# Weight sums of the Strassen pairs: additions alone, and two of the four made by DMA in the feed-forward

## The chip, the cores and the metric

One core of one Trainium2 chip. The metric is the device time of one execution in microseconds, the median of three. Matrix work runs on TensorE (PE), elementwise work on VectorE (DVE) and ScalarE (ACT); GpSimd (POOL) and SyncE (SP) mostly issue DMAs. All data is float32.

## The reference

One layer of a hybrid encoder over a prompt of 512 rows and 8 sample streams of 16 rows (T = 640 rows together, 1024 columns): three gated branches are merged, and a SwiGLU feed-forward of width 2816 follows. The part that matters here:

```python
z = x @ w_in                                  # among its columns: the gates of the branches
g = jax.nn.sigmoid(gates + b_gate)
x = layer_norm(ALPHA * x + merged @ w_out, ln1_g, ln1_b)
ffn = (jax.nn.silu(x @ w_ffn_gate) * (x @ w_ffn_up)) @ w_ffn_down
x = layer_norm(ALPHA * x + ffn, ln2_g, ln2_b)
```

## The kernel before, in words

Activations lie transposed in SBUF, 128 features by rows, split for precision into a high part `xh` (fp32r) and a low part `xl`. A weight block is split the same way just before use: ACT copies the high part, DVE subtracts it from the block to get the low part. Each product is then three matmuls: high by high, high by low, low by high.

**The work as a list of steps.** The program is one list `steps`, written out in a fixed order. A step has a weight part, its matmuls (`mm`), an evacuation, and work to be done ahead of it (`before`). The order of the code sets the order on each engine: for step i the high part of step i + 2 is copied, `before` runs, the matmuls run, and between them come the evacuation of step i - 1 and the low split of step i + 2. Weight loads of 1 MB (`Load`) go out on the SP queue into two buffers `wr`. The next load is issued when the low split of the last step that reads the old buffer is in the program, and it waits on the chip for that split.

**Strassen pairs.** Two column blocks of a weight matrix (256 columns, one load) make a `Pair`. Its 1024 by 256 block is cut in four quarters 11, 12, 21, 22 (128 partitions by 512 elements each) and the activations in four as well. Seven products m1, m6, m2, m7, m5, m4, m3 of 12 matmuls each (128x320) take the place of eight. They need four sums of weight quarters, t1 to t4, each 128x512, and four sums of activations, s1 to s4. DVE forms the weight sums of a pair while the pair before it is multiplied: t3 and t2 (`sums_1`) ahead of step 2, t1 and t4 (`sums_2`) ahead of step 3 (one step later in the first pair of a run of pairs). The products gather in PSUM: m6 and m7 share a bank, and m6's value is read by DVE between the two (`after`).

Eight pairs make gates of the branches (`gate_pairs`), and twenty make the feed-forward: for each two blocks a "gate" pair (`through`, Silu on ACT) and an "up" pair (`times`, a multiplication on DVE). `seven` writes the seven steps of a pair, `pair_steps` a run of pairs. Below, the twenty are counted from 0. Temporary tiles come from 53 slots of 128x640 in a first-in, first-out list (`get`, `free`).

`Engine` only counts assumed times, for the order of side work; in the feed-forward pairs there is none. L66 is the line that records every operation of PE, ACT and DVE, so instructions are told by their tiles: `wr` the load's buffer, `wh` and `wl` the split blocks (two buffers in turn, each with both parts), `pu` PSUM, `s` any slot.

Of the kernel before, what the change touches and what calls it, by code (L numbers as in the profile page):

```python
# [11 lines left out]
OP = mybir.AluOpType  # L12
# [133 lines left out]
def trunk(ctx, tc, x_prompt, x_sample, mem_t, rows_a, rows_b, hist_b, cache_k, cache_v, ln_in_g, ln_in_b, w_in,  # L146
# [69 lines left out]
    class Load:  # L216
        def __init__(self, shape, ap, users):
            self.shape, self.ap, self.left, self.tile = shape, ap, users, None
            loads.append(self)
# [1168 lines left out]
    def sums_stream(in_place=None, given=None):  # L1388

        quarters.clear()  # L1390
        for n, (t0, k0) in QUARTERS.items():
            quarters[n] = tuple([x[:, k0 + k, t0:t0 + HT] for k in range(half)] for x in (xh, xl))
        a = {}

        def whole(n, i):
            t0, k0 = QUARTERS[n]
            if given is not None:
                a[n, i] = given.pop((t0 // HT, (k0 + i) // 2))
                return
            a[n, i] = get([128, 2, HT])  # L1400
            V.tensor_tensor(a[n, i], *(f32(x[:, k0 + i:k0 + i + 2, t0:t0 + HT]) for x in (xh, xl)), op=OP.add)

        def mix(out, p, q, i, op=OP.subtract):
            V.tensor_tensor(a[out, i], a[p, i], a[q, i], op=op)

        def part(n, q, keep=False):

            at = [], []
            for i in blocks:
                hi, lo = get([128, 2, HT], F32R), get([128, 2, HT], F32R)  # L1410
                split(hi, lo, a[q, i])
                if not keep:
                    free(a.pop((q, i)))
                sums.extend((hi, lo))
                for to, y in zip(at, (hi, lo)):
                    to.extend(y[:, k] for k in range(2))
                yield "v"
            quarters[n] = at
            made.add(n)

        blocks = range(0, half, 2)
        for i in blocks:
            whole("22", i)
            whole("21", i)
            yield "v"
            mix("22", "21", "22", i, OP.add)
            whole("11", i)
            yield "v"
            mix("21", "11", "21", i)
            mix("11", "22", "11", i)  # L1430
            yield "v"
        yield from part("s2", "11", True)
        if in_place is None:
            yield from part("s1", "22")
        yield from part("s3", "21")
        for i in blocks:
            whole("12", i)
            yield "v"
            mix("12", "12", "11", i)
            free(a.pop(("11", i)))  # L1440
            yield "v"
        yield from part("s4", "12")
        if in_place is not None:
            while not in_place():
                yield None
            for i in blocks:
                split(*(y[:, i:i + 2, HT:] for y in (xh, xl)), a["22", i])
                free(a.pop(("22", i)))
                yield 1
            quarters["s1"] = quarters.pop("21")  # L1450
            made.add("s1")
# [14 lines left out]
    class Pair:  # L1466


        def __init__(self, ld):
            self.ld, self.t = ld, {}  # L1470

        def block(self, n):
            if n[0] == "t":
# [1 line left out]
            i, j = int(n[0]) - 1, int(n[1]) - 1  # L1475
            return self.ld.tile[:, j, half * i:half * (i + 1)]

        def add(self, n, p, q, op):
            self.t[n] = get([128, half, 128])
            V.tensor_tensor(self.t[n], self.block(p), self.block(q), op=op)  # L1480

        def sums_1(self):
            self.add("t3", "22", "12", OP.subtract)
            self.add("t2", "t3", "11", OP.add)

        def sums_2(self):
            self.add("t1", "12", "11", OP.subtract)
            self.add("t4", "t2", "21", OP.subtract)

        def drop(self, n):  # L1490
            if n in self.t:
# [4 lines left out]
                ("m3", "z", False, "s4", "22"))  # L1496
    parity = [0]

    def seven(pair, put, following, first=False):

        acc, tmp, late = {}, {}, []

        def fourth(p):
            put(0, 1, p, tmp["b"][:, 0], OP.subtract)

        def fifth(p):
            put(1, 1, p, tmp["b"][:, 0], OP.add)
            if first:
                V.tensor_tensor(tmp["a"][:, 1], tmp["a"][:, 1], p, op=OP.add)

        def after(n, p):
            if n == "m1":
                tmp["a"], tmp["b"] = get([128, 2, HT]), get([128, 2, HT])
                copy(tmp["a"][:, 0], p)
            elif n == "m6":
                V.tensor_tensor(tmp["a"][:, 1], tmp["a"][:, 0], p, op=OP.add)
            elif n == "m2":
                put(0, 0, p, None, None)
            elif n == "m7":
                V.tensor_tensor(tmp["b"][:, 0], tmp["a"][:, 0], p, op=OP.add)  # L1520
                for f in late:
                    f()
            elif n in ("m4", "m5"):
                f = lambda: (fourth if n == "m4" else fifth)(p)
                if first:
                    late.append(f)
                else:
                    f()
            else:
                free(tmp["b"])  # L1530
                put(1, 0, p, tmp["a"][:, 1], OP.add)
                free(tmp["a"])

        products = PRODUCTS
        if first:

            products = [PRODUCTS[i] for i in (0, 5, 2, 1, 4, 3)] + [("m3", "x", True, "s4", "22")]
        for i, (n, u, opens, xn, wn) in enumerate(products):
            def mm(w, u=u, opens=opens, xn=xn):
                if opens:  # L1540
                    acc[u] = pu(1)[0][:, :HT]
                p = acc[u]
                hi, lo = w
                xhi, xlo = quarters[xn]
                for k in range(half):
                    P.matmul(p, hi[:, k], xhi[k], start=opens and k == 0, stop=False, skip_group_check=not opens)
                    P.matmul(p, hi[:, k], xlo[k], start=False, stop=False, skip_group_check=not opens)
                yield
                for k in range(half):
                    P.matmul(p, lo[:, k], xhi[k], start=False, stop=k == half - 1, skip_group_check=not opens)  # L1550
                yield

            before = None
            if first:
                wanted = "s1" if i == 1 else xn if xn[0] == "s" else None
                ahead = following and {3: following.sums_1, 4: following.sums_2}.get(i)
                before = lambda wanted=wanted, ahead=ahead: (wanted and sums_for(wanted), ahead and ahead())
            elif following and not first and i == 2:
                before = following.sums_1
            elif following and not first and i == 3:  # L1560
                before = following.sums_2
            Step(pair.ld, (lambda r, wn=wn: pair.block(wn)), [128, half, 128], mm,
                 (lambda n=n, u=u: after(n, acc[u])), before=before, half=parity[0] % 2,
                 after=lambda wn=wn: pair.drop(wn))
            parity[0] += 1

    def pair_steps(pairs, start=True):

        early = steps[-2]
        ahead = early.before  # L1570
        early.before = lambda: (ahead and ahead(), pairs[0][0].sums_1(), pairs[0][0].sums_2())
        for i, (pair, put) in enumerate(pairs):
            seven(pair, put, pairs[i + 1][0] if i + 1 < len(pairs) else None, start and i == 0)

    def w_load(w, col, users):
        return Load([128, 2, KD, 128], lambda: blocks_of(w[col // 256], 2), users)
# [1 line left out]
    def through(function, to, ready=None, **how):  # L1578

        def put(j, c, p, x, op):  # L1580
            row = to(j)
            h = c2(row)[:, c]
            if x is not None:
                V.tensor_tensor(h, x, p, op=op)
            A.activation(h, p if x is None else h, function, **{n: f(j) for n, f in how.items()})
            if ready and j != c:
                ready(j, row)
        return put
# [256 lines left out]
    def times(m2):  # L1845

        def put(j, c, p, x, op):
            h = c2(hT[m2 + j])[:, c]
            y = p
            if x is not None:  # L1850
                y = get([128, HT])
                V.tensor_tensor(y, x, p, op=op)
            V.tensor_tensor(h, h, y, op=OP.mult)
            if x is not None:
                free(y)
        return put

    pairs = []
    for m2 in range(2, KF, 2):
        pairs.append((Pair(w_load(w_ffn_gate, m2 * 128, 7)),  # L1860
                      through(AF.Silu, lambda i, m2=m2: slot_of(hT, m2 + i))))
        pairs.append((Pair(w_load(w_ffn_up, m2 * 128, 7)), times(m2)))
    pair_steps(pairs)
    for k in range(2):
        assert steps[-5 + k].before is None
# [279 lines left out]
```

## Time and profile before

| | before |
|---|---|
| median of 3 runs | 1041.67 us (1041.48 to 1042.96) |
| profiled execution | 1041.37 us, span 1039.6 us |
| granted TensorE clock | 0.997 |
| POOL's share of the span | 10% |
| moved by DMA | 142.00 MB, 137 GB/s mean |
| feed-forward pairs | about 628 to 884 us of the span |

Times in the trace are microseconds from the span's start. A row of the order of time reads: start, duration, engine, line, operation, out<-in, shapes, count, and in brackets the idle time before it with what ended it. Matmuls are pipelined, so each shows a longer duration than the distance to the next. A row of DMA issues reads: queue, count, KB, and the us from issue to landing.

### The profile page before, as it was taken

What the parts mean: (1) busy time and instruction counts of PE and PEld (TensorE: products, weight loads), DVE (VectorE), ACT (ScalarE), POOL (GpSimd) and SP (SyncE); (2) the same over time, 40 slices, a digit from 0 to 9 for tenths busy, and PEclk for the clock granted to TensorE, in tenths of its full rate; (3) what the DMA queues carried; (4) which work ended last, traced back from release to release, by engine and by line L of the source; (5) the groups of instructions that cost most, each with busy time, mean ns of one, the idle gap of its engine ahead of it and who ended that gap; (6) DMA issues with size and microseconds to landing.
All of it is one profiled execution on the core that took longest, in us unless ns stands there. A gap on an engine that the chain in (4) does not pass through costs nothing.

```text
span 1039.6 us, 16847 instructions
## 1 busy us (share of the span) xinstructions
PE 1028.0 (99%) x6641; PEld 978.2 (94%) x6641; DVE 819.2 (79%) x1452; ACT 517.2 (50%) x938; POOL 99.9 (10%) x176
## 2 busy tenths in 40 slices
PE   9999999999999999999999999999999999999997
PEld 6999999999999999999998899999999999888886
DVE  5769899899953969898785579888888887576875
ACT  5723564356579686755322455444444334344350
POOL 1000403110100010101021210000000001000111
PEclk9999999999999999999999999999999999999998
DMA  9722215641240154844566222222222223833581
GB/s 350 256 89 82 79 61 174 220 162 62 92 169 24 42 183 157 203 107 151 186 241 218 102 102 81 82 82 81 81 85 95 101 87 115 310 122 122 183 283 41
DMA packets 34590, 142.00 MB, mean 137 GB/s; under 512 B 4656, under 2 KB 5488, under 8 KB 24656
## 3 DMA queue, kind: packets, MB, share of 16 engines
q1 hardware_dynamic: 23472, 104.84, 28.8%
q0 software_dynamic: 11040, 36.10, 10.6%
q8 instruction: 52, 0.85, 0.3%
q14 instruction: 26, 0.21, 0.1%
HBM read 120.55 MB, written 20.36 MB: 136 GB/s over the span
## 4 chain that ended last, share of the span: by engine, by line
PE 94%; DVE 3%; ACT 1%; issue 1%; DMA 1%; DVEq 0%; POOL 0%; POOLq 0%; SPq 0%
PE pu L66 83%; PE pv L66 11%; DVE s L66 2%; ACT s L66 1%; DMA wr<-in_w_in 1%; DVE wl L66 1%; DVE wh L66 0%; DVE xres L66 0%; ACT wh L66 0%; ACT L66 0%; DVEq L2141 0%; ACT xh L66 0%; ACT wl L66 0%; DVE st L66 0%; ACT hout L66 0%
## 5 line engine op out<-in xcount | busy, mean ns | idle before, releaser
L66 ACT ACTIVATE wh<-wr 128x1024 fp32r<-128x1024 f32 (+1 forms) x147 | 130.1, 888 | 200.0 <-PE pu L66 100.8
L66 PE MATMUL pu<-xh,wh 128*128 128x320 f32 x976 | 228.9, 310 | 0.5 <-ACT xh L66 0.5
L66 PE MATMUL pu<-xh,wl 128*128 128x320 f32 x976 | 227.7, 309 | 0.1
L66 PE MATMUL pu<-s,wh 128*128 128x320 f32 x1136 | 196.4, 309 | 1.1 <-ACT s L66 1.0
L66 PE MATMUL pu<-xl,wh 128*128 128x320 f32 x792 | 193.7, 309 | 0.0
L66 DVE TENSOR_TENSOR s<-s,s 128x640 f32<-128x640 f32 (+5 forms) x206 | 144.2, 721 | 46.8 <-ACT s L66 44.3
L66 PEld LDWEIGHTS pu<-s,wh 128*128 128x128 f32 x1136 | 174.0, 188 | 1.8 <-ACT s L66 1.3
L66 PEld LDWEIGHTS pu<-xh,wh 128*128 128x128 f32 x976 | 164.9, 188 | 2.4 <-issue 1.0
L66 PEld LDWEIGHTS pu<-xh,wl 128*128 128x128 f32 x976 | 165.4, 188 | 0.4 <-DVE wl L66 0.4
L66 PE MATMUL pu<-s,wl 128*128 128x320 f32 x880 | 158.6, 309 | 1.1 <-DVE s L66 1.1
L66 DVE TENSOR_TENSOR wl<-wr,wh 128x1024 fp32r<-128x1024 f32 (+1 forms) x105 | 119.2, 1138 | 48.3 <-ACT wh L66 48.3
L66 PEld LDWEIGHTS pu<-s,wl 128*128 128x128 f32 x880 | 136.3, 188 | 1.8 <-issue 1.1
L66 PEld LDWEIGHTS pu<-xl,wh 128*128 128x128 f32 x792 | 136.4, 188 | 0.0
L66 DVE TENSOR_TENSOR s<-s,pu 128x320 f32<-128x320 f32 x192 | 91.1, 485 | 51.1 <-PE pu L66 47.7
L66 ACT ACTIVATE s<-s 128x640 fp32r<-128x640 f32 (+4 forms) x148 | 89.3, 627 | 79.1 <-DVE s L66 77.5
L66 DVE SCALAR_TENSOR_TENSOR s<-s,pb,s 128x511 f32<-128x511 f32 (+14 forms) x240 | 111.9, 533 | 5.8 <-ACT s L66 5.8
L66 PE MATMUL pu<-wh,s 128*128 128x512 f32 x364 | 106.7, 382 | 0.0
L66 PEld LDWEIGHTS pu<-wh,s 128*128 128x128 f32 x364 | 67.0, 188 | 13.3 <-issue 0.5
L66 ACT ACTIVATE s<-pu 128x320 f32<-128x320 f32 (+2 forms) x110 | 44.3, 437 | 64.0 <-PE pu L66 63.4
L66 PE MATMUL pu<-s,s 128*128 128x512 f32 (+1 forms) x236 | 61.8, 413 | 0.0
L66 PE MATMUL pu<-wl,s 128*128 128x512 f32 x182 | 57.1, 381 | 0.0
L66 PEld LDWEIGHTS pu<-s,s 128*128 128x128 f32 x236 | 43.1, 190 | 14.0 <-issue 7.0
(127 smaller groups left out, 1203.3 us busy)
## 6 DMA issues: line engine op xcount, KB each, us to landing
wr<-in_w_in SPq DMA_DIRECT2D x26, 1024.0 KB, 4.9
wr<-in_w_ffn_down SPq DMA_DIRECT2D x19, 1024.0 KB, 4.8
wr<-in_w_ffn_gate SPq DMA_DIRECT2D x11, 1024.0 KB, 4.8
wr<-in_w_ffn_up SPq DMA_DIRECT2D x11, 1024.0 KB, 4.7
m<-s POOLq DMA_DIRECT2D x16, 320.0 KB, 4.9
s<-in_cache_k POOLq DMA_DIRECT2D x16, 256.0 KB, 5.3
s<-in_cache_v POOLq DMA_DIRECT2D x16, 256.0 KB, 5.0
wr<-in_proj_a SPq DMA_DIRECT2D x4, 1024.0 KB, 5.5
```

Source lines behind the costliest of these rows:

```text
L66: return f(*a, **k)
```

## The change

The sums are written so that all four weight sums are additions (t3 = 22 + 12, t2 = t3 + 11, t1 = 12 + 11, t4 = t2 + 21). For that some signs change sides: in the activation sums and in the evacuations, where the PSUM operand now comes first.

In the feed-forward, for every pair but the first, t3 and t1 are no longer formed by DVE. `fetch` loads quarters 22 and 11 once more from memory into the slots of t3 and t1 (SP queue, 256 KB each). `gather` then adds quarter 12 to each by an accumulating DMA (POOL queue, 256 KB each). `sums_1` and `sums_2` skip what is there, so t2 = t3 + 11 and t4 = t2 + 21 stay on DVE at their places. `fetch` of pair i + 2 stands ahead of step 5 of pair i, `gather` ahead of its step 6; those of pair 1 stand three and two steps ahead of pair 0.

```diff
     class Pair:
...
-        def add(self, n, p, q, op):
+        def add(self, n, p, q):
+            if n in self.t:
+                return
             self.t[n] = get([128, half, 128])
-            V.tensor_tensor(self.t[n], self.block(p), self.block(q), op=op)
+            V.tensor_tensor(self.t[n], self.block(p), self.block(q), op=OP.add)
+
+        def in_memory(self, n):
+            i, j = int(n[0]) - 1, int(n[1]) - 1
+            return self.ld.ap()[:, j, half * i:half * (i + 1)]
+
+        def fetch(self):
+            for n, q in (("t3", "22"), ("t1", "11")):
+                self.t[n] = get([128, half, 128])
+                S.dma_start(self.t[n], self.in_memory(q))
+
+        def gather(self):
+            for n in ("t3", "t1"):
+                G.dma_start(self.t[n], self.in_memory("12"), accum_op=OP.add)
 
         def sums_1(self):
-            self.add("t3", "22", "12", OP.subtract)
-            self.add("t2", "t3", "11", OP.add)
+            self.add("t3", "22", "12")
+            self.add("t2", "t3", "11")
 
         def sums_2(self):
-            self.add("t1", "12", "11", OP.subtract)
-            self.add("t4", "t2", "21", OP.subtract)
+            self.add("t1", "12", "11")
+            self.add("t4", "t2", "21")
...
-    def seven(pair, put, following, first=False):
+    def seven(pair, put, following, first=False, second=None):
...
         def fourth(p):
-            put(0, 1, p, tmp["b"][:, 0], OP.subtract)
+            put(0, 1, p, tmp["b"][:, 0], OP.add)
...
+            wanted = (("s1" if i == 1 else xn if xn[0] == "s" else None) if first else None)
+            ahead = []
+            if following:
+                ahead += {2 + first: [following.sums_1], 3 + first: [following.sums_2]}.get(i, [])
+            if second:
+                ahead += {5: [second.fetch], 6: [second.gather]}.get(i, [])
             before = None
...
+            if wanted or ahead:
+                before = lambda wanted=wanted, ahead=ahead: (wanted and sums_for(wanted), [f() for f in ahead])
...
+        pairs += [(None, None)] * 2
+        pre = pairs[1][0].summed
+        earlier(3, *([pairs[1][0].fetch] if pre else []))
+        earlier(2, pairs[0][0].sums_1, pairs[0][0].sums_2, *([pairs[1][0].gather] if pre else []))
...
-                V.tensor_tensor(h, x, p, op=op)
+                V.tensor_tensor(h, p, x, op=op)
...
-        pairs.append((Pair(w_load(w_ffn_gate, m2 * 128, 7)),
+        pairs.append((Pair(w_load(w_ffn_gate, m2 * 128, 7), True),
...
-        pairs.append((Pair(w_load(w_ffn_up, m2 * 128, 7)), times(m2)))
+        pairs.append((Pair(w_load(w_ffn_up, m2 * 128, 7), True), times(m2)))
```

On DVE, in pair 5, from the sums for pair 6 to the low split of m3. Before (the numbers behind `s` are the slot and a running count; in brackets the engines and DMA queues, HW for SP and SW for POOL, that the instruction waits for):

```order
L66 TENSOR_TENSOR s27_513_7763<-wr_7682 128x512 [waits DMAHW2_49]
L66 TENSOR_TENSOR s48_514_7765<-s27_513_7763,wr_7682 128x512 [waits DVE_49]
L66 TENSOR_TENSOR s7_511_7753<-s7_511_7753,pu_7744 128x320 [waits PE_49,Activation_49]
L66 TENSOR_TENSOR wl_7761<-s5_507_7650,wl_7761 128x512 [waits Activation_49]
L66 TENSOR_TENSOR s4_515_7783<-wr_7682 128x512
L66 TENSOR_TENSOR s47_516_7785<-s48_514_7765,wr_7682 128x512 [waits DVE_49]
L66 TENSOR_TENSOR s24_509_7662<-s24_509_7662,pu_7726 128x320 [waits PE_49]
L66 TENSOR_TENSOR wh_7781<-s6_508_7652,wh_7781 128x512 [waits Activation_49]
L66 TENSOR_TENSOR s51_512_7754<-s7_511_7753,pu_7744 128x320 [waits PE_49]
L66 TENSOR_TENSOR wl_7801<-wr_7547,wl_7801 128x512 [waits Activation_49]
```

and now:

```order
L66 TENSOR_TENSOR s47_515_7779<-s48_510_7700,wr_7692 128x512 [waits DMAHW4_49,DMASW3_49]
L66 TENSOR_TENSOR s51_513_7769<-s51_513_7769,pu_7760 128x320 [waits PE_49,Activation_49]
L66 TENSOR_TENSOR wl_7777<-s13_501_7565,wl_7777 128x512 [waits DMASW2_49,Activation_49]
L66 TENSOR_TENSOR s44_516_7797<-s47_515_7779,wr_7692 128x512 [waits DVE_49]
L66 TENSOR_TENSOR s24_509_7672<-s24_509_7672,pu_7742 128x320 [waits PE_49]
L66 TENSOR_TENSOR wh_7795<-s38_508_7662,wh_7795 128x512 [waits Activation_49]
L66 TENSOR_TENSOR s36_514_7770<-s51_513_7769,pu_7760 128x320 [waits PE_49]
L66 TENSOR_TENSOR wl_7813<-wr_7555,wl_7813 128x512 [waits Activation_49]
```

The first rows of t3 and t1 (`s27` and `s4` from `wr` alone) are gone. t2 (`s48` before, `s47` now) waits for the accumulating DMA besides its weight load. It still stands ahead of the read of m6 (`s7` before, `s51` now, from `pu`). The read of m7 and, last, m3's low split from `wr` keep their places.

On the SP queue, from the load of pair 4 on, before:

```order
L255 DMA wr_7415<-in_w_ffn_gate 128x2048 [waits DMAHW6_49,DVE_49]
L255 DMA wr_7547<-in_w_ffn_up 128x2048 [waits DMAHW7_49,DVE_49]
L255 DMA wr_7682<-in_w_ffn_gate 128x2048 [waits DMAHW0_49,DVE_49]
L255 DMA wr_7814<-in_w_ffn_up 128x2048 [waits DMAHW1_49,DVE_49]
L255 DMA wr_7949<-in_w_ffn_gate 128x2048 [waits DMAHW2_49,DVE_49]
```

and now, from the load of pair 4 to that of pair 7:

```order
L255 DMA wr_7421<-in_w_ffn_gate 128x2048 [waits DMAHW6_49,DMAHW0_49,DVE_49]
L1491 DMA s1_493_7429<-in_w_ffn_gate 128x512 [waits DMASW3_49,DMASW2_49]
L1491 DMA s31_494_7431<-in_w_ffn_gate 128x512
L255 DMA wr_7555<-in_w_ffn_up 128x2048 [waits DMAHW3_49,DMAHW1_49,DVE_49]
L1491 DMA s41_500_7563<-in_w_ffn_up 128x512 [waits DMAHW2_49]
L1491 DMA s13_501_7565<-in_w_ffn_up 128x512
L255 DMA wr_7692<-in_w_ffn_gate 128x2048 [waits DMAHW6_49,DMAHW4_49,DVE_49]
L1491 DMA s48_510_7700<-in_w_ffn_gate 128x512 [waits DMAHW5_49]
L1491 DMA s0_511_7702<-in_w_ffn_gate 128x512 [waits Pool_49]
L255 DMA wr_7826<-in_w_ffn_up 128x2048 [waits DMAHW7_49,DMAHW1_49,DVE_49]
```

Each pair's two fetches stand directly behind its own weight load. On POOL, where nothing stood between the last store of x1 and the load of the residual, there are now 38 accumulations:

```order
L1495 DMA s1_493_7429<-in_w_ffn_gate 128x512 [waits DMAHW7_49,DMASW7_49,DVE_49]
L1495 DMA s31_494_7431<-in_w_ffn_gate 128x512 [waits DMAHW0_49,DMASW0_49,DVE_49]
L1495 DMA s41_500_7563<-in_w_ffn_up 128x512 [waits DMAHW2_49,DMASW1_49,DVE_49]
L1495 DMA s13_501_7565<-in_w_ffn_up 128x512 [waits DMAHW3_49,DMASW2_49,DVE_49]
L1495 DMA s48_510_7700<-in_w_ffn_gate 128x512 [waits DMAHW5_49,DMASW3_49,DVE_49]
L1495 DMA s0_511_7702<-in_w_ffn_gate 128x512 [waits DMAHW6_49,DMASW4_49,DVE_49]
```

Each waits for its fetch (DMAHW). The order on PE and the number of instructions on ACT stay as they were.

More of the change, by code (lines that the diff above doesn't have):

```diff
@@ L1425, in sums_stream @@
             yield "v"
-            mix("22", "21", "22", i, OP.add)
+            mix("22", "21", "22", i)
             whole("11", i)
@@ L1438, in sums_stream @@
             yield "v"
-            mix("12", "12", "11", i)
+            mix("12", "12", "11", i, OP.add)
             free(a.pop(("11", i)))
@@ L1466, in trunk, with __init__ @@
     class Pair:
-        def __init__(self, ld):
-            self.ld, self.t = ld, {}
+        def __init__(self, ld, summed=False):
+            self.ld, self.t, self.summed = ld, {}, summed
         def block(self, n):
@@ L1497, in trunk @@
     parity = [0]
-    def seven(pair, put, following, first=False):
+    def seven(pair, put, following, first=False, second=None):
         acc, tmp, late = {}, {}, []
         def fourth(p):
-            put(0, 1, p, tmp["b"][:, 0], OP.subtract)
+            put(0, 1, p, tmp["b"][:, 0], OP.add)
         def fifth(p):
-            put(1, 1, p, tmp["b"][:, 0], OP.add)
+            put(1, 1, p, tmp["b"][:, 0], OP.subtract)
             if first:
-                V.tensor_tensor(tmp["a"][:, 1], tmp["a"][:, 1], p, op=OP.add)
+                V.tensor_tensor(tmp["a"][:, 1], tmp["a"][:, 1], p, op=OP.subtract)
         def after(n, p):
@@ L1530, in after @@
                 free(tmp["b"])
-                put(1, 0, p, tmp["a"][:, 1], OP.add)
+                put(1, 0, p, tmp["a"][:, 1], OP.subtract)
                 free(tmp["a"])
@@ L1551, in mm @@
                 yield
-            before = None
[L1554 to L1561, printed above, removed]
+            wanted = (("s1" if i == 1 else xn if xn[0] == "s" else None) if first else None)
[4 more added lines that the diff above has]
+                ahead += {5: [second.fetch], 6: [second.gather]}.get(i, [])
+            before = None
+            if wanted or ahead:
+                before = lambda wanted=wanted, ahead=ahead: (wanted and sums_for(wanted), [f() for f in ahead])
             Step(pair.ld, (lambda r, wn=wn: pair.block(wn)), [128, half, 128], mm,
@@ L1567, in pair_steps, with earlier @@
     def pair_steps(pairs, start=True):
[L1569 to L1573, printed above, removed]
+        def earlier(n, *jobs):
+            s = steps[-n]
+            ahead = s.before
+            s.before = lambda: (ahead and ahead(), [f() for f in jobs])
+        pairs += [(None, None)] * 2
+        pre = pairs[1][0].summed
+        earlier(3, *([pairs[1][0].fetch] if pre else []))
+        earlier(2, pairs[0][0].sums_1, pairs[0][0].sums_2, *([pairs[1][0].gather] if pre else []))
+        for i in range(len(pairs) - 2):
+            pair, put = pairs[i]
+            second = pairs[i + 2][0]
+            seven(pair, put, pairs[i + 1][0], start and i == 0, second if second and second.summed else None)
     def w_load(w, col, users):
@@ L1851, in put @@
                 y = get([128, HT])
-                V.tensor_tensor(y, x, p, op=op)
+                V.tensor_tensor(y, p, x, op=op)
             V.tensor_tensor(h, h, y, op=OP.mult)
```

## The prediction

> **What bounds the kernel now.** I read the page's busy shares first, then the busy time by stage, then the chain that ended last, and last the order of time inside one pair of the feed-forward.
>
> ```profile
> PE 1028.0 (99%) x6641; PEld 978.2 (94%) x6641; DVE 819.2 (79%) x1452; ACT 517.2 (50%) x938; POOL 99.9 (10%) x176
> 366.00:446.00 80.00, 78.18 (x527) 77.02 (x525) 66.93 (x111) 58.32 (x103) 11.06 (x16) 1.00 0.61 180
> 628.00:641.00 13.00, 13.00 (x91) 13.00 (x90) 12.93 (x21) 7.80 (x15) 0.00 (x0) 1.00 0.18 75
> 641.00:653.00 12.00, 12.00 (x84) 12.00 (x83) 11.22 (x22) 6.54 (x14) 0.00 (x0) 1.00 0.25 89
> 665.00:865.00 200.00, 200.00 (x1366) 200.00 (x1365) 164.17 (x292) 84.05 (x163) 0.00 (x0) 1.00 0.24 85
> 627.76 256.18 PE pu L66 x1740
> ```
>
> The first row is the whole span, the next four are stages (length, then PE, PEld, DVE, ACT, POOL, granted clock, DMA share, GB/s), the last is one piece of the chain. In the feed-forward pairs, 628 to 884 us, the chain is 1740 matmuls in 256.18 us without a break. DVE is busy there (164.17 of 200 us; 12.93 of 13 in the first pair), yet PE waits for nothing. So DVE time taken out of this stage is worth nothing by itself; only a new wait can change it. The gate pairs (366 to 446 us), where PE does idle 1.8 us, keep all their instructions.
>
> Inside one pair (number 5 from zero, an "up" pair), on DVE, PE and the SP queue:
>
> ```profile
> 691.56 0.68 DVE L66 TENSOR_TENSOR wh<-wr,wh 128x512 fp32r<-128x512 f32 x1
> 698.59 0.69 DVE L66 TENSOR_TENSOR s<-wr 128x512 f32<-128x512 f32 x1
> 699.31 0.69 DVE L66 TENSOR_TENSOR s<-s,wr 128x512 f32<-128x512 f32 x1
> 700.02 0.49 DVE L66 TENSOR_TENSOR s<-s,pu 128x320 f32<-128x320 f32 x1
> 703.47 0.49 DVE L66 TENSOR_TENSOR s<-s,pu 128x320 f32<-128x320 f32 x1 [0.15 <-PE pu L66]
> 703.88 0.69 DVE L66 TENSOR_TENSOR wl<-wr,wl 128x512 fp32r<-128x512 f32 x1
> 701.51 1.92 PE L66 MATMUL pu<-s,wh 128*128 128x320 f32 x12
> 703.27 1.92 PE L66 MATMUL pu<-s,wl 128*128 128x320 f32 x12
> 692.27 0.33 SPq L255 DMA_DIRECT2D wr<-in_w_ffn_gate  x1
> 704.59 0.33 SPq L255 DMA_DIRECT2D wr<-in_w_ffn_up  x1
> ```
>
> A product starts every 1.76 us (701.51 to 703.27), a pair takes 12.32 us (692.27 to 704.59 between two weight loads). The loads have two buffers: the low split of m3's block (691.56, 703.88) is the last reader of the old one, and the next load leaves 0.03 us after it ends. At 698.59 and 699.31 DVE forms t3 and t2 of the pair to come. Right behind, at 700.02, it reads m6 out of PSUM; m7, at 701.51, adds into that same bank and must wait for this read, which ended at 700.51. That margin of 1.0 us is what the change spends.
>
> **The change part by part.** (a) Signs and operand order. The sums are as many and as large; a subtraction becomes an addition. In the evacuations the PSUM operand now comes first.
>
> ```profile
> L66 DVE TENSOR_TENSOR s<-s,pu 128x320 f32<-128x320 f32 x192 | 91.1, 485 | 51.1 <-PE pu L66 47.7
> L66 DVE TENSOR_TENSOR s<-pu,s 128x320 fp32r<-128x320 f32 x8 | 3.5, 485 | 1.0 <-ACT s L66 1.0
> L66 DVE TENSOR_TENSOR s<-wr 128x512 f32<-128x512 f32 x56 | 38.3, 684 | 0.9 <-DMA wr<-in_w_in 0.9
> L66 DVE TENSOR_TENSOR s<-s,wr 128x512 f32<-128x512 f32 x56 | 38.5, 688 | 1.0
> ```
>
> Both orders take 485 ns: 0 us.
>
> (b) Removed from DVE: t3 and t1 in 19 of the 20 feed-forward pairs, 38 sums of 684 ns, 26 us of DVE time. PE has no gap there, so 0 us.
>
> (c) Added to SP: 38 fetches of 256 KB, each pair's two right behind its own weight load. The program takes about nine slots a pair and has at least nine free at each fetch, so a fetch's slot was given back over a pair earlier and SP doesn't wait for it. Behind the two fetches on SP stands the next weight load, 12 us later: 0 us there.
>
> (d) Added to POOL: 38 accumulating DMAs of 256 KB, each waiting for its fetch to land. POOL does nothing else in these 256 us (0.00 in the stage rows); what is queued behind the last is the residual's load, due only after the pairs: 0 us there.
>
> (e) The new wait. t2 = t3 + block 11 stays on DVE and is still ahead of m6's read, but t3 now exists only when weight load, fetch and accumulation have gone by one after the other. Call L the time from a pair's weight load to the landing of its t3. m7 starts on time if t2 starts by 701.51 - 0.05 - 1.20 = 700.26 (t2 start to the end of m6's read is 0.71 + 0.49 us, from the rows at 699.31 and 700.02), that is L up to 700.26 - 692.27 = 8.0 us. Beyond, it is a loop: t3 lands, t2 and m6's read (1.20), m7 (0.05 + 1.76), its read (0.20 after the end, 0.41 to the next), m3's low split (0.68), load issue (0.03): 4.3 us; in up pairs DVE, catching up, comes 0.1 later, so 4.4 on the mean. A pair then takes L + 4.4 instead of 12.32 us.
>
> What L is. Nearest rows for load and fetch: a load with two SP loads of 320 KB right behind it, and the rate at which they ran.
>
> ```profile
> 400.72 0.33 SPq L255 DMA_DIRECT2D wr<-in_w_in  x1
> 401.16 0.85 SPq L1106 DMA_DIRECT2D s<-b  x2
> wr<-in_w_in SPq DMA_DIRECT2D x1, 1024.0 KB, 4.8
> s<-b SPq DMA_DIRECT2D x1, 320.0 KB, 5.2
> 405.00:406.00 1.00, 1.00 (x9) 1.00 (x8) 0.83 (x2) 1.00 (x4) 0.00 (x0) 1.00 0.99 389
> ```
>
> The first of the two landed at 401.16 + 5.2 = 406.36, 5.64 us after the load's issue; 64 KB less at 389 GB/s is 0.17 less, so t3's fetch lands at 5.5. The load itself had landed at 4.8: the queue works in order, no overlap.
>
> The accumulation into SBUF is not in this trace. Nearest are accumulations of 320 KB from SBUF into m (442.50, two in a row; 418.08, with loads beside it), plain stores of the same (276.22), and plain loads of 256 KB on POOL (236.89):
>
> ```profile
> 442.50 1.75 POOL L1101 DMA_DIRECT2D m<-s  x2 [11.60 <-DVE s L66]
> m<-s POOLq DMA_DIRECT2D x1, 320.0 KB, 4.6
> 418.08 0.85 POOL L1101 DMA_DIRECT2D m<-s  x1 [0.48 <-DVE s L66]
> m<-s POOLq DMA_DIRECT2D x1, 320.0 KB, 7.5
> 276.22 0.54 POOL L1101 DMA_DIRECT2D m<-s  x1 [4.36 <-DVE ve L66]
> m<-s POOLq DMA_DIRECT2D x1, 320.0 KB, 2.4
> 236.89 0.54 POOL L1239 DMA_DIRECT2D s<-in_lru_w  x1 [11.26 <-PE pv L66]
> s<-in_lru_w POOLq DMA_DIRECT2D x1, 256.0 KB, 3.0
> ```
>
> Lower end 3.0 us, a load without any adding; upper end 7.5. The nearest in kind is the pair at 442.50: first of two, queue otherwise empty, 4.6. Against a plain store adding costs 4.6 - 2.4 = 2.2 us, by 256/320 some 1.7; upon the plain load that is 4.7; the 4.6 shrunk the same way is about 4.1. I take 4.4. With 0.1 us for POOL to react (estimate) L = 5.5 + 0.1 + 4.4 = 10.0 us: 2.0 over the margin. Ends: 8.6 and 13.1.
>
> [...]
>
> **Sum.** t2 of pairs 2 to 19 waits so, 18 times (pair 1's sums are fetched some 20 us ahead). The first of these hangs on pair 0:
>
> ```profile
> 643.89 0.68 DVE L66 TENSOR_TENSOR wh<-wr,wh 128x512 fp32r<-128x512 f32 x1
> 652.23 1.92 PE L66 MATMUL pu<-s,wh 128*128 128x320 f32 x12
> ```
>
> DVE is late in pair 0, and two sums fewer (1.2 us) free the buffer at about 643.4; t3 lands at 653.4, m7 begins at 654.65 instead of 652.23: 2.4 us. The other 17 cost L + 4.4 - 12.32 = 2.1 us each, 35.4. Together +38 us. The profiled execution took 1041.37 us (span 1039.6), 0.3 under the median of 1041.67, so 1079 us.
>
> **Rivals.** *In time* (not slower): t3 lands within 8.0 us of its load, the accumulation in 2.4 us. For it speaks only the plain store at 2.4; no load on POOL was under 3.0. Then PE stays unbroken, since 26 us less DVE work frees nothing that PE waits for: 1041. It decides at L = 8.0, and a DVE wait below that is swallowed by the 1.0 us margin.
>
> *Cheap adding*: the landing costs more than a plain store's 2.4 us and up to 3.7: L of 8.0 to 9.3, up to 1.4 us a pair, 18 times: 1042 to 1066, and 1054 at the plain load's 3.0. The rows at 442.50 speak against it, though they write to memory and not to SBUF. [...]
>
> *Dear adding*: the two accumulations of a pair share the engines, or the second fetch delays the first of them, and it lands like the one at 418.08, 5.6 to 7.5 us. L of 11.2 to 13.1, 3.3 to 5.2 us a pair: +59 to +94, 1100 to 1135. Against it: one pair's transfers are past when t3's accumulation begins; nothing else loads then.
>
> *Faster*: would need a PE wait that DVE's relief ends. In this stage there is none; I see no mechanism and leave it a rest.
>
> **How the numbers follow.** The wait with 3.7 to 5.6 us (1066 to 1100): 0.62. Cheap: 0.15. Dear: 0.11. In time: 0.08. Faster: 0.04. Less than 0.2% (2.1 us) this kernel's runs can hardly tell from no change. So faster 0.04, same 0.08, slower 0.88. The range 1049 to 1110 leaves out the last two, the cheapest of the cheap and some of the dear: 0.2.
>
> **What would show it.** After the change the chain of the feed-forward stage should no longer be one unbroken PE piece: DVE should wait for a DMA into a slot in each pair, some 3 us ahead of the 128x512 sum, and PE some 2 us for DVE ahead of the first matmul of m7; weight loads should leave every 14.4 us, and the stage's DVE time should fall by 26 us. Accumulations of 256 KB should land 4.4 us after their issue. I am wrong if weight loads still leave every 12.3 us, if the fetches land sooner than 5.5 us after the load, or if PE's stops lie at another product.

## The result, and the profile after

| | before | after |
|---|---|---|
| median | 1041.68 us (1041.11 to 1042.96, 6 runs) | 1086.73 us (1080.77 to 1093.04, 6 runs) |
| profiled execution | 1041.37 us, span 1039.6 | 1082.17 us, span 1080.3 |
| moved by DMA | 142.00 MB | 161.94 MB |

The change makes the kernel slower: ratio 1.0433, 95% interval 1.0387 to 1.0478. The spread of its runs grew too, from 1.9 to 12.3 us. The forecast was 1079 (1049 to 1110), slower.

The page's busy shares after, the feed-forward stage (length, PE, PEld, DVE, ACT, POOL, clock, DMA share, GB/s), the whole list of PE's waits, and DVE's waits for DMAs:

```profile
PE 1034.2 (96%) x6641; PEld 979.4 (91%) x6641; DVE 794.0 (73%) x1414; ACT 516.6 (48%) x938; POOL 133.6 (12%) x214
641.00:925.00 284.00, 249.69 (x1653) 244.38 (x1652) 175.68 (x318) 103.33 (x198) 36.23 (x45) 0.99 0.53 145
PE pu L66 <- DVE s L66: 35.4, 21, 3.5
PE pu L66 <- DVE ident L66: 1.4, 1, 1.4
PE pu L66 <- ACT s L66: 1.0, 1, 1.0
PE pu L66 <- ACT xh L66: 0.5, 1, 0.5
DVE s L66 <- DMA s<-in_w_ffn_gate: 33.9, 9, 5.3
DVE s L66 <- DMA s<-in_w_ffn_up: 33.5, 9, 4.3
```

DVE is 25 us less busy (794.0 against 819.2) and TensorE is busy in 249.69 of 284 us where it had no gap. DVE now waits 9 + 9 times for an accumulated slot. PE waits 35.4 us for DVE, 34.3 more than before. The chain of the stage was one piece of 256.18 us; around one pair it now reads (at the dots, rows between t2 and m6's read are left out):

```profile
703.16 0.33 SPq L255
703.49 0.06 issue
703.54 5.06 DMA s<-in_w_ffn_gate
708.61 0.02 issue
708.63 0.04 POOLq L1495
708.67 0.49 issue
709.17 3.82 DMA s<-in_w_ffn_gate
712.99 0.02 issue
713.01 0.04 DVE s L66
...
713.62 0.49 DVE s L66
714.11 0.04 issue
714.16 7.32 PE pu L66 x48
```

Weight load (703.16), fetch (5.06 us), POOL (0.56 us from the fetch's landing at 708.61), accumulation (3.82 us), t2 on DVE (713.01), the read of m6 (713.62), m7 on PE (714.16): the loop of the prediction. In the next pair the profile puts POOL's wait down to a DVE split:

```profile
723.39 1.77 POOL L1495 DMA_DIRECT2D s<-in_w_ffn_up  x2 [12.44 <-DVE wh L66]
717.77 0.85 SPq L1491 DMA_DIRECT2D s<-in_w_ffn_up  x2
s<-in_w_ffn_up SPq DMA_DIRECT2D x1, 256.0 KB, 5.1
```

The fetch had landed there too some 0.5 us before POOL began (717.77 + 5.1 = 722.9), so the loop is the same. The place at 713 us on DVE and PE, and the loads:

```profile
713.01 0.69 DVE L66 TENSOR_TENSOR s<-s,wr 128x512 f32<-128x512 f32 x1 [3.44 <-DMA s<-in_w_ffn_gate]
713.62 0.48 DVE L66 TENSOR_TENSOR s<-s,pu 128x320 f32<-128x320 f32 x1
716.63 0.68 DVE L66 TENSOR_TENSOR wl<-wr,wl 128x512 fp32r<-128x512 f32 x1
714.16 2.03 PE L66 MATMUL pu<-s,wh 128*128 128x320 f32 x12 [1.59 <-DVE s L66]
716.02 1.92 PE L66 MATMUL pu<-s,wl 128*128 128x320 f32 x12
658.88 0.33 SPq L255 DMA_DIRECT2D wr<-in_w_ffn_up  x1
703.16 0.33 SPq L255 DMA_DIRECT2D wr<-in_w_ffn_gate  x1
717.34 0.33 SPq L255 DMA_DIRECT2D wr<-in_w_ffn_up  x1
891.13 0.33 SPq L255 DMA_DIRECT2D wr<-in_w_ffn_up  x1
```

DVE stands idle for 3.44 us before t2, PE for 1.59 us before m7, and m3's low split at 716.63 sends the next load at 717.34, 14.18 us after the last one. From 658.88 to 891.13 sixteen such periods take 14.52 us on the mean (12.32 before).

### The profile page after: what moved, and what is told of

Its sections match the earlier page's. It is cut to its first block, busy times and chain, and to the rows that moved or that the text cites. A ratio compares the mean times of both kernels' runs of the same rounds, so it can differ in the third digit from the quotient of the medians.

```text
span 1080.3 us, 16990 instructions
## 1 busy us (share of the span) xinstructions
PE 1034.2 (96%) x6641; PEld 979.4 (91%) x6641; DVE 794.0 (73%) x1414; ACT 516.6 (48%) x938; POOL 133.6 (12%) x214
## 2 busy tenths in 40 slices
DMA packets 45536, 161.94 MB, mean 150 GB/s; under 512 B 5872, under 2 KB 6704, under 8 KB 35600
## 4 chain that ended last, share of the span: by engine, by line
PE 77%; DMA 11%; DVE 5%; issue 3%; ACT 2%; SPq 0%; DVEq 0%; POOL 0%; POOLq 0%; ACTq 0%
PE pu L66 67%; PE pv L66 10%; DMA s<-in_w_ffn_gate 7%; DMA s<-in_w_ffn_up 3%; DVE s L66 3%; ACT s L66 1%; DVE wh L66 1%; DVE wl L66 1%; DMA wr<-in_proj_a 1%; DMA s<-in_w_mem_k 1%; DMA pa<-in_rows_a 0%; ACT wh L66 0%; DVE st L66 0%; DVE xl L66 0%; SPq L255 0%
## 5 line engine op out<-in xcount | busy, mean ns | idle before, releaser
L66 DVE TENSOR_TENSOR s<-s,wr 128x512 f32<-128x512 f32 x56 | 38.5, 688 | 67.7 <-DMA s<-in_w_ffn_gate 33.9
L66 DVE TENSOR_TENSOR s<-pu,s 128x320 f32<-128x320 f32 (+1 forms) x92 | 44.5, 489 | 32.3 <-PE pu L66 28.7
L66 DVE TENSOR_TENSOR s<-s,pu 128x320 f32<-128x320 f32 x108 | 50.3, 481 | 18.8 <-PE pu L66 18.6
```

Source lines behind the costliest of these rows:

```text
L66: return f(*a, **k)
```

## The experiments

My theory: the whole loss is t2's wait for its accumulated t3, closed into a loop through the weight buffer. Rivals: the new signs and operand order; the 20 MB of extra traffic and POOL's work; only the order of t2 and m6's read. All eight runs start from the changed kernel; their ratios are to runs of the kernel before on the same chip.

**The signs alone.**

```diff
-        pairs.append((Pair(w_load(w_ffn_gate, m2 * 128, 7), True),
+        pairs.append((Pair(w_load(w_ffn_gate, m2 * 128, 7)),
...
-        pairs.append((Pair(w_load(w_ffn_up, m2 * 128, 7), True), times(m2)))
+        pairs.append((Pair(w_load(w_ffn_up, m2 * 128, 7)), times(m2)))
```

> The sums and evacuations in their new signs and operand order, but all four weight sums of every pair on DVE, no fetch and no accumulation. Theory (the whole loss is t2's wait for its accumulated t3): 1041.5 us, within 0.2% of before. Rival (the new signs or the PSUM operand first cost something): above 1044.

1041.44 us, ratio 1.0003 (0.9993 to 1.0013). The additions in their new form cost nothing; all of the loss is in the DMA part.

**The same DMAs a pair earlier.**

```diff
-                ahead += {5: [second.fetch], 6: [second.gather]}.get(i, [])
+                ahead += {1: [second.fetch], 2: [second.gather]}.get(i, [])
```

> As after the change, but the fetches of pair i + 2 stand ahead of step 1 of pair i and the accumulations ahead of step 2 (before: steps 5 and 6), so that on SP they go out behind the weight load of the pair before and not behind their own; same DMAs, same bytes, same DVE work. Theory: t3 has landed long before t2 asks for it, the loop is open, 1041.5 us, and the spread of the runs is small again. Rival (20 MB more DMA traffic and POOL's descriptors slow PE, DVE or the loads): still 1070 or more.

1041.95 us, ratio 1.0006 (0.9997 to 1.0016), runs within 1.4 us. Its chain through the stage, and the stage's busy times:

```profile
627.49 256.19 PE pu L66 x1740
641.00:881.00 240.00, 240.00 (x1638) 239.96 (x1638) 175.15 (x315) 101.51 (x195) 31.37 (x37) 1.00 0.59 163
```

The chain is again 1740 matmuls in 256.19 us, with the DMAs at 163 GB/s and POOL at 31 us. The weight loads land after 4.8 and 4.9 us at the median (4.8 and 4.7 before). Traffic and POOL's work slow nothing that PE waits for here; the rival falls. And DVE's relief earns nothing either, as the prediction had it.

**t2 one step later.** Behind m6's read, but still ahead of the low split that frees the weight buffer.

```diff
-                ahead += {2 + first: [following.sums_1], 3 + first: [following.sums_2]}.get(i, [])
+                late_by = 1 if following.summed else 0
+                ahead += {2 + first + late_by: [following.sums_1], 3 + first + late_by: [following.sums_2]}.get(i, [])
```

> As after the change, but DVE's t2 stands one step later (t4 as well), so behind the read of m6, yet still ahead of m7's read and m3's low split that frees the weight buffer. Theory of the loop (load, fetch, accumulation, t2, low split, load): m7 is free, but from t3's landing to the next load DVE still does 3.2 us of work (4.4 before), so a pair takes some 13.1 to 13.3 us instead of 12.32: 1054 to 1059. Rival (only the order of t2 and m6's read counts, PE waiting for the PSUM bank): 1041.5.

1056.64 us, ratio 1.0149 (1.0134 to 1.0164). DVE's t2, m3's low split and the next load:

```profile
706.20 0.69 DVE L66 TENSOR_TENSOR s<-s,wr 128x512 f32<-128x512 f32 x1 [2.44 <-DMA s<-in_w_ffn_gate]
708.81 0.69 DVE L66 TENSOR_TENSOR wl<-wr,wl 128x512 fp32r<-128x512 f32 x1
696.47 0.33 SPq L255 DMA_DIRECT2D wr<-in_w_ffn_gate  x1
709.52 0.33 SPq L255 DMA_DIRECT2D wr<-in_w_ffn_up  x1
```

A load leaves 13.05 us after the last one (13.24 on the mean of sixteen), 3.3 us after t2 began. The PSUM bank is out of the way and a third of the loss remains: it is the loop, not that bank alone, that sets the pace.

**t2 behind the split.**

```diff
-                ahead += {2 + first: [following.sums_1], 3 + first: [following.sums_2]}.get(i, [])
+                if following.summed and not first:
+                    ahead += {5: [following.sums_1], 6: [following.sums_2]}.get(i, [])
+                else:
+                    ahead += {2 + first: [following.sums_1], 3 + first: [following.sums_2]}.get(i, [])
```

> As after the change, but DVE's t2 stands three steps later, behind m3's low split. Theory of the loop: t3 may land up to 12.3 us after its weight load, it lands after about 9.9, the loop is open: 1041.5 us. Rival (a late t2 delays m6 of the next pair, or contention): above 1044.

1041.10 us, ratio 1.0001 (0.9991 to 1.0010). DVE's list of waits holds no wait for a slot loaded in this stage any more, and PE's wait for DVE is back at 1.1 us. The DMAs are as late as after the change: at the median of both DMAs of a pair the fetches land 5.2 us (gate) and 5.3 us (up) after their issue (5.3 and 5.3 after the change), the accumulations after 4.9 and 4.5 us (4.9 and 4.5). Nobody waits for them.

**The adding left out.**

```diff
         def gather(self):
             for n in ("t3", "t1"):
-                G.dma_start(self.t[n], self.in_memory("12"), accum_op=OP.add)
+                G.dma_start(self.t[n], self.in_memory("12"))
```

> As after the change, but POOL's second DMA is a plain load of quarter 12 over the fetched quarter, still waiting for the fetch: the adding is left out, so t3 and t1 are quarter 12 alone; bytes and waits stay. Theory: the landing after POOL's issue falls from about 3.8 us to about 3.0 (the plain load of the trace before), the loop shortens by 0.8 us a pair, some 14 us less than after the change: 1062 to 1071. Rival (adding costs nothing, the price is the second DMA's fixed time): as after the change, 1080 or more. Rival (adding is most of it): 1050 or less.

1073.16 us, ratio 1.0308 (1.0284 to 1.0332): 2 us above the band, 14 us under the change. The first landing of a pair, with the adding (after the change, at 709.17) and without (here, at 720.28):

```profile
s<-in_w_ffn_gate POOLq DMA_DIRECT2D x1, 256.0 KB, 3.8
s<-in_w_ffn_up POOLq DMA_DIRECT2D x1, 256.0 KB, 3.3
PE pu L66 <- DVE s L66: 25.3, 21, 2.7
```

Landings were 3.6 to 3.9 us with the adding (two of 18 took 4.6 and 5.7) and as a rule 3.3 to 3.4 without (all 18 between 2.8 and 3.8). PE's wait for DVE, the third line, fell from 35.4 to 25.3 us, 0.56 a stop. So adding costs about half a microsecond and not the 0.8 expected, some 10 us in 18 pairs. That the medians lie 14 us apart, as the theory had it, is in part luck: the profiled executions lie 7.8 us apart, and the clock, treated at the end, fell once after the change and twice here. Seven tenths of PE's added wait stay with a plain second load (24.2 of 34.3 us), because the second DMA comes after the first at all.

**Only t1 by DMA, only t3 by DMA.** The first:

```diff
-            for n, q in (("t3", "22"), ("t1", "11")):
+            for n, q in (("t1", "11"),):
...
-            for n in ("t3", "t1"):
+            for n in ("t1",):
```

> Only t1 is fetched and accumulated, t3 is formed by DVE as before the change. Theory (only t3 has a reader on DVE that comes too soon; t1 is first read a pair later): 1041.5 us. Rival (any accumulation in the stage costs): half of the loss, 1060.

1041.34 us, ratio 1.0003 (0.9994 to 1.0012). The second has "t3" and "22" in these places:

> Only t3 is fetched and accumulated, t1 is formed by DVE, in its old place behind t2. Theory: the loop as after the change, with one sum of DVE (0.6 us) more between t3's landing and the next load: at least the loss of after the change, 1085 to 1098. Rival (the two accumulations of a pair delay each other): less loss than after, 1075 or less.

1088.07 us, ratio 1.0450 (1.0432 to 1.0468), with half of the transfers. All of the loss hangs on t3. Whether the one sum more on DVE costs something can't be read from 1088.07 against 1086.73, given the spread of the changed kernel, but it can be read from the trace, where t1's sum stands between t2 and the next load:

```profile
712.59 0.69 DVE L66 TENSOR_TENSOR s<-s,wr 128x512 f32<-128x512 f32 x1 [2.61 <-DMA s<-in_w_ffn_gate]
714.20 0.69 DVE L66 TENSOR_TENSOR s<-wr 128x512 f32<-128x512 f32 x1
717.51 0.33 SPq L255 DMA_DIRECT2D wr<-in_w_ffn_up  x1
```

From t2's start to the next load it is 4.92 us here (712.59 to 717.51) and 4.33 after the change (713.01 to 717.34), so in this pair the sum costs the expected 0.6. In the pairs between these it is 0.2: 4.55 us from t3's landing to the next load (727.72 to 732.27) against 4.35. The 727.72 is an estimate: m7's start at 728.89 less the 1.17 us from t3's landing to m7's start after the change (712.99 to 714.16).

**The fetches without the adding DMA.**

```diff
         def gather(self):
-            for n in ("t3", "t1"):
-                G.dma_start(self.t[n], self.in_memory("12"), accum_op=OP.add)
+            pass
```

> The fetches stay, the accumulations are left out, so t3 is quarter 22 alone and t1 quarter 11 alone. Theory: t3 lands 5.6 us after the pair's load is issued, under the 8.0 us that m7 allows, no wait: 1041.5 us. Rival (the fetches behind the load delay it and with it DVE): above 1044.

1041.53 us, ratio 1.0003 (0.9994 to 1.0013). The fetches behind the pair's own load land 5.2 us (gate) and 5.3 us (up) after their issue at the median, and PE's wait for DVE is 1.3 us (1.1 before): loads alone come in time. It takes the second, dependent DMA (9.8 us after the change) to pass the 8.0 us.

## Why the prediction was right

Direction, mechanism and place held: steps (a) to (d) were free, and step (e), the wait of t2, was the loss, with PE's restarts and clock as its consequences. Point by point, from the profiled execution:

- *The loop's fixed part* (4.3 to 4.4 us): 717.34 - 712.99 = 4.35.
- *The fetch* (5.5 us after the load): 708.61 - 703.16 = 5.45. The row of a load with two others behind it gave the right price, and queue order: the load itself had landed 4.8 us after its issue, ahead of the fetch. By its letter one sign of being wrong did come, a fetch landing sooner than 5.5 us after the load: at 759.92 it took 5.35 (760.29 + 4.98 = 765.27). The sign had been set on the forecast itself, with no room for scatter; the other two, loads every 12.3 us and stops at another product, did not come.
- *The accumulation* (4.4 us, from stores into memory): 3.6 to 3.9 in 16 of 18. I had put it 0.6 too high, since adding costs about 0.5 us here and not the 1.7 taken from the stores. The lowest load of 256 KB on POOL before was not 3.0 us: one at 198.16 landed after 2.9.
- *POOL's reaction* (0.1 us, an estimate that no run shows): 0.56 us from the fetch's landing to the accumulation's start (708.61 to 709.17), 0.81 in one pair (664.54 to 665.35). Too low by nearly 0.5, which nearly cancels the former. That is luck: with the landing as measured and POOL's 0.1, L would have been 9.4 and the sum 18 times 1.4, +26 us, at the upper end of the rival with cheap adding.
- *L*: 9.8 us in a common period against 10.0.
- *A pair* (14.4 us): 14.1 to 14.3 in the common periods, 14.52 on the mean. What I left out is that the parts scatter: fetches of 5.0 to 5.7 us, accumulations of 4.6 and 5.7. In the loop such a delay is paid in full: the accumulation of 5.7 us, 1.9 over the usual 3.8, stands in the longest period, 16.06 us (875.07 to 891.13) against 14.18.
- *PE's stops* (2.1 us a pair, 2.4 the first): the 2.1 is what a period grows by, 2.2 on the mean, and a stop shows less idle time than that. In the pair above the period grew by 14.18 - 12.32 = 1.86 us, with PE idle for 1.59: the row of the last matmul before the stop reaches into it, and the first product behind it takes 1.86 us (714.16 to 716.02) instead of 1.76. The idle time of the 18 stops is 34.3 us, the first 3.36 (its fetch took 6.4 us). The other 6.4 us of the 40.7 by which the span grew are PE's restarts, some 0.27 us a stop (an estimate from this pair), and its clock, below, with 1.55.

The sum gave +38 us. The profiled execution has +40.8, the median +45; the six runs lie between +39 and +51. The forecast put nothing down for TensorE's clock, which the last section treats; the four longest of the six runs are those in which it was lowest.

## What to carry to other kernels

Before work is taken off an engine, look whether anything waits for that engine in that stage: here PE had no gap in 256 us, so 25 us less of DVE could earn nothing, in the change as in the variants that wait for nothing. The sum made by two DMAs, one after the other, landed here 9.8 us after the pair's load was issued: 5.45 to the fetch's landing, 0.56 for POOL, 3.82 for the accumulation. Put the reader of such a sum that much later (or the fetch earlier), and check what stands behind the reader in its engine's order, above all if that frees the buffer from which the next round starts.

## What was not expected of the hardware

TensorE's granted clock fell after some of the stops. After the change it happened once, to 0.67 behind a stop of 2.01 us. With the adding left out it happened in two places, behind stops of 1.91 and 2.66 us (to be seen in rows of 2.91 to 3.57 us for twelve matmuls instead of 1.92 to 2.03); with only t3 by DMA in six, behind stops of 1.88 to 3.61 us, to 0.57 at the lowest in stretches of 4 us. PE's steps after the change, then a stretch with the clock (length, PE, clock, DMA share, GB/s):

```profile
670.29 2.83 PE L66 MATMUL pu<-s,wl 128*128 128x320 f32 x12 [2.01 <-DVE s L66]
672.92 2.71 PE L66 MATMUL pu<-s,wh 128*128 128x320 f32 x12
887.94 2.03 PE L66 MATMUL pu<-s,wh 128*128 128x320 f32 x12 [3.46 <-DVE s L66]
672.00:676.00 4.00, 4.00 (x21) 0.67 0.25 31
```

Two steps took 5.17 us (670.29 to 675.46) instead of the 3.62 behind another stop (714.16 to 717.78), so this drop cost 1.55 us. A stop of 3.46 us that ended at 887.94 was followed by full speed (1.00 from 888 to 892 us). The length of a stop alone does not tell whether the clock falls: in these runs it fell behind one of 1.88 us and not behind this one. What else decides is not shown.

The spread of the changed kernel's runs goes with this clock. Over the whole execution it was 0.997 and 0.994 in the two shortest of the six runs (1082.17 and 1080.77 us) and 0.987 to 0.990 in the four others (1084.64 to 1093.04). With t2 one step later the loop was closed as well, but the clock stayed at 0.998 or 0.999 in all four runs, and they lay within 1.7 us. The kept trace is of the run at 0.997; that the others lost their time at further falls of the clock is likely, but not shown.
